# One level of Strassen's algorithm for the two wide products of a SwiGLU block

## The chip, the core and the metric

The kernel runs on one core of a Trainium2 chip. The core has five engines with an instruction stream each: PE (TensorE, matmuls and transposes, results in PSUM), DVE (VectorE), ACT (ScalarE), POOL (GpSimd) and SP (SyncE, which here only issues DMAs). Sixteen DMA engines move data between DRAM and SBUF. The metric is the device time of one execution in microseconds (us), the median over runs. All data are float32.

## What is computed

One decoder block on 512 tokens of 2048 channels. Cut to the parts that matter:

```
h = rmsnorm(x, norm1_g) * (1 + scale1(c)) + shift1(c)
x = x + gate1(c) * (mixer(h) @ w_out)              # mixer begins with h @ w_in
h = rmsnorm(x, norm2_g) * (1 + scale2(c)) + shift2(c)
x = x + gate2(c) * ((silu(h @ w_ff1) * (h @ w_ff3)) @ w_ff2)
out = rmsnorm(x, norm_f_g)
# w_ff1, w_ff3: 2048 x 5632; w_ff2: 5632 x 2048; scale, shift, gate: parts of silu(c) @ w_ada + b_ada
```

The products with w_ff1, w_ff3 and w_ff2 are 70% of the multiplications with large weights.

## The kernel before

A large product is a stream of units (`stream`). A unit is 1 MB of weights, loaded by one DMA on SP's queue into `ws` (2 buffers, pool `wsp`), and 48 matmuls of a 128x128 by a 128x512 tile in 16 steps. Each float32 operand is split in two: a high part that ScalarE casts (L75) and a low part that VectorE subtracts (L76). A product is then three matmuls, high by high, high by low and low by high (`mm3`). While a unit runs, the weights of the next are split, 512 columns after every fourth step, into `wh` and `wl` (5 buffers each); so a load, a cast, a subtraction and the matmuls run beside each other, and the buffers tie them together.

The program has a head (x, the first norm, the first two parts of w_ada, the first columns of w_in), then units for w_in with the mixer in lanes between the steps (`Lane`: small jobs that advance by a step every few steps of the stream), then w_out, then the feed-forward part. `cols_head` loads small rows and transposes them on TensorE (L141) in the head.

The feed-forward part: `open_h2` and `make_h2` transpose x (16 blocks of channels, four transposes each, L1049), scale it by the norm and split it into 16 slots `xh`, `xl`. Four blocks are made before the first product, the other twelve among the first units. `ff_units` then takes 8 (once 4) of the 44 blocks of 128 hidden channels at a time. `block_unit` computes 4 blocks of h @ w_ff1 or h @ w_ff3 with the weights stationary and all 512 tokens moving, 4 units for 512 columns of either weight; the results come out with channels on partitions, go through silu and the product (`d1`, `d3`, L1087) and are split into `hid` (8 buffers in SBUF). Then `row_unit` computes these blocks of hidden @ w_ff2, tokens on partitions, and `add_row` multiplies the sums by the gate and adds them to x (L909, L910) after each group of blocks. In PSUM the eight banks are `row`. The gate's columns, `ada(5, cc)`, run in a lane that begins with the feed-forward part: 16 loads of 256 KB (`wa`) and 16 operations on VectorE for 512 columns. The rstd of the tokens is spread over the partitions by matmuls with a diagonal (`dg`, `rstd_rows`) and applied in `make_h2`.

A scheduler orders each engine's instructions from this program; buffers are tiles of pools, and a tile waits until the last use of the one that had its buffer.

## Time and profile before

| | |
|---|---|
| median of 3 runs | 2545.15 us (2540.65 to 2547.0) |
| span of the profiled execution | 2543.8 us |
| PE busy | 2463.2 us (97%), 14344 matmuls |
| DVE busy | 1441.2 us (57%) |
| ACT busy | 901.1 us (35%) |
| POOL busy | 100.0 us (4%) |
| DMA | 336.32 MB, mean 132 GB/s |

The profiled execution is one of its own, recorded by the hardware profiler; its span runs from its first to its last instruction. Busy times of the engines overlap. Matmuls are pipelined: the busy time of one (0.39 us) is longer than the distance between two, so the price of a matmul is read from a run of many. The stages lie at about 0 to 140 us (head), 140 to 930 us (w_in and the mixer), 930 to 1078 us (the end of the mixer and w_out) and 1086 us to the end (feed-forward).

### The profile page before, as it was taken

To read this page: it belongs to the slowest core of one execution; us is meant where nothing else is said; L and a number is where in the kernel's file an instruction comes from. 1 tells how busy PE (TensorE), PEld (TensorE's weight loads), DVE (VectorE), ACT (ScalarE), POOL (GpSimd) and SP (SyncE) were. 2 spreads that over 40 slices of the span, in tenths; PEclk is the share of its full clock that TensorE was granted. 3 is DMA by queue.
4 is the path that set the end of the run, shared out by engine and by line. 5 is a ranking of instruction groups with operands and counts; after the bars stand their busy time and mean duration, and the time that the engine had idled before them with its cause. 6 is when DMAs were issued, how large, how long until landed. Compare 5 with 4: busy or idle time off the path is not lost.

```text
span 2543.8 us, 35816 instructions
## 1 busy us (share of the span) xinstructions
PE 2463.2 (97%) x14344; PEld 1943.0 (76%) x14344; DVE 1441.2 (57%) x2553; ACT 901.1 (35%) x1461; POOL 100.0 (4%) x157
## 2 busy tenths in 40 slices
PE   6999899999999999999999999999999999999998
PEld 5767666776776767788888888888888888888886
DVE  5765888888988876686343443244324322342345
ACT  4354355356446442342222222222222222222323
POOL 2011110010010000000000000000000000000000
PEclk9999999999999999999999999999999999999999
DMA  9953344344444567556323333322332322233323
GB/s 339 346 164 84 105 117 123 93 125 139 108 107 137 183 207 227 191 190 219 122 91 99 99 100 99 96 88 98 100 99 100 99 90 94 99 100 100 99 98 114
DMA packets 275686, 336.32 MB, mean 132 GB/s; under 512 B 35619, under 2 KB 157713, under 8 KB 274496
## 3 DMA queue, kind: packets, MB, share of 16 engines
...
HBM read 321.41 MB, written 12.58 MB: 131 GB/s over the span
## 4 chain that ended last, share of the span: by engine, by line
PE 85%; DVE 7%; DMA 4%; ACT 2%; issue 1%; POOL 1%; DVEq 0%; ACTq 0%; SPq 0%; POOLq 0%
PE row L67 60%; PE acc L67 14%; PE bk L67 5%; DMA wa<-in_w_ada_dram 3%; PE gg L67 2%; DVE cy L839 1%; DVE wl L76 1%; PE fp L67 1%; PE yy L67 1%; PE first L67 1%; DVE ada L878 1%; DVE tmp L697 0%; ACT L206 0%; DMA dd<-D16d 0%; PE bk L635 0%
## 5 line engine op out<-in xcount | busy, mean ns | idle before, releaser
L76 DVE TENSOR_TENSOR wl<-ws,wh 128x512 fp32r<-128x512 f32 x740 | 519.8, 707 | 847.6 <-ACT wh L75 805.5
L75 ACT CAST wh<-ws 128x512 fp32r<-128x512 f32 x740 | 458.7, 621 | 1288.0 <-PE row L67 1059.7
L67 PE MATMUL row<-xh,wh 128*128 128x512 f32 x1408 | 550.7, 391 | 0.0
L67 PE MATMUL row<-xh,wl 128*128 128x512 f32 x1408 | 548.2, 389 | 0.0
L67 PE MATMUL row<-xl,wh 128*128 128x512 f32 x1408 | 548.1, 389 | 0.0
L67 PE MATMUL row<-wh,hid 128*128 128x512 f32 x1408 | 434.6, 389 | 0.0
L67 PEld LDWEIGHTS row<-xl,wh 128*128 128x128 f32 x1408 | 264.4, 188 | 55.5 <-issue 1.0
L67 PEld LDWEIGHTS row<-xh,wh 128*128 128x128 f32 x1408 | 264.4, 188 | 55.0 <-issue 1.0
L67 PEld LDWEIGHTS row<-xh,wl 128*128 128x128 f32 x1408 | 264.3, 188 | 55.1
L67 PEld LDWEIGHTS row<-wh,hid 128*128 128x128 f32 x1408 | 264.3, 188 | 55.0 <-ACT hid L75 0.2
L67 PE MATMUL row<-wl,hid 128*128 128x512 f32 x704 | 274.0, 389 | 0.0
L67 PE MATMUL acc<-xh,wh 128*128 128x512 f32 x592 | 258.1, 436 | 2.8 <-ACT wh L75 2.8
L67 PE MATMUL acc<-xl,wh 128*128 128x512 f32 x592 | 241.6, 408 | 0.0
L67 PE MATMUL acc<-xh,wl 128*128 128x512 f32 x592 | 239.1, 404 | 0.0
L878 DVE SCALAR_TENSOR_TENSOR ada<-wa,sc,ada 128x512 f32<-128x512 f32 x256 | 191.7, 749 | 52.1 <-DMA wa<-in_w_ada_dram 46.8
L67 PEld LDWEIGHTS row<-wl,hid 128*128 128x128 f32 x704 | 132.2, 188 | 27.4
L67 PEld LDWEIGHTS acc<-xh,wh 128*128 128x128 f32 x592 | 111.9, 189 | 35.1 <-issue 5.1
L67 PEld LDWEIGHTS acc<-xh,wl 128*128 128x128 f32 x592 | 112.4, 190 | 26.5 <-issue 1.9
L67 PEld LDWEIGHTS acc<-xl,wh 128*128 128x128 f32 x592 | 112.5, 190 | 24.7 <-issue 5.7
L206 ACT ACT_TABLE_LOAD x85 | 109.1, 1283 | 2.3 <-PEq L1213 0.8
L839 DVE SCALAR_TENSOR_TENSOR cy<-cu,colC,cy 128x512 f32<-128x512 f32 x120 | 96.6, 805 | 1.7
L839 DVE SCALAR_TENSOR_TENSOR cy<-cu,colD,cy 128x512 f32<-128x512 f32 x120 | 89.2, 744 | 0.6
...
## 6 DMA issues: line engine op xcount, KB each, us to landing
ws<-in_w_ff_dram SPq DMA_DIRECT2D x132, 1024.0 KB, 5.2
wa<-in_w_ada_dram SPq DMA_DIRECT2D x256, 256.0 KB, 3.0
ws<-in_w_in_dram SPq DMA_DIRECT2D x37, 1024.0 KB, 5.9
wa<-in_w_ada_dram SPq DMA_DIRECT2D x32, 1024.0 KB, 11.5
ws<-in_w_out_dram SPq DMA_DIRECT2D x8, 1024.0 KB, 5.1
wa<-in_x_dram SPq DMA_DIRECT2D x4, 1024.0 KB, 6.1
x<-in_x_dram SPq DMA_DIRECT2D x4, 1024.0 KB, 10.7
...
```

The source lines that it names most:

```text
L67: return self.nc.tensor.matmul(out, lhsT=lhsT, rhs=rhs, start=start, stop=stop, skip_group_check=True)
L75: self.nc.scalar.copy(out=hi, in_=x)
L76: self.nc.vector.tensor_tensor(out=lo, in0=x, in1=hi.bitcast(F32), op=ALU.subtract)
L206: self.last_fn = nc.scalar.preload_act_table_set(name).ins
L839: v.scalar_tensor_tensor(out=y, in0=u[:, t:t + T], scalar=self.tap(t, b), in1=y, op0=ALU.mult, op1=ALU.add)
L878: nc.vector.scalar_tensor_tensor(out=acc, in0=was[r], scalar=self.sc[:, r:r + 1], in1=acc, op0=ALU.mult, op1=ALU.add)
```

## The change

The products with w_ff1 and w_ff3 are made by one level of Strassen's algorithm in Winograd's form. The 2 x 2 blocks are: tokens in halves of 256; channels of x in even and odd blocks of 128; columns by weight, 512 of w_ff1 and the same 512 of w_ff3. Seven products of blocks give the four results. In code:

- `make_a`, `make_b` make the sums and differences of x, split (three products' operands in `make_a`, four in `make_b`); x is already scaled by its norm when it is transposed, so the matmuls with the diagonal are gone. Transposes of x stay 64.
- `Fast` is the new unit. It loads 1 MB of w_ff1 (`ws2`, 3 buffers, `WS2`) and 1 MB of w_ff3 (`ws`, 2 buffers) and forms differences of the two on VectorE. Part 0 has 3 products (12 steps, 36 matmuls), part 1 has 4 (16 steps, 48 matmuls); each part has 4 units for 512 columns, and both parts load the same weights. x is now stationary and the weights move. A split is 128x1024 (two blocks of 512) into `pair` (3 buffers of each), started two products ahead.
- `end0`, `end1` combine the products on VectorE and write two of the partial sums back into PSUM, where the products of part 1 add to them. Results have tokens on partitions; `turn` transposes them (16 transposes for 512 columns), splits them and writes both parts to DRAM (`hidd`) through POOL's queue, from the same three buffers `wa` that w_ada uses. The last four blocks stay in SBUF.
- The products with w_ff2 come after all of this, in three passes of 12, 16 and 16 blocks; `back` reads hidden blocks from DRAM through POOL's queue. `add_row` runs after each pass. x goes to DRAM (`x1d`) in the meantime, and `ada(5, cc)` begins with w_ff2.
- The pools of weights lie on the other side of SBUF (`side="right"`).

```diff
+    def bank(self, n):
+        return self.rowp.tile([P, 512], F32, name="b%d" % n, bufs=1)
...
+    def pair(self):
+        return [self.w.tile([P, 2, 512], F32R, name=n, bufs=3) for n in ("wh", "wl")]
...
-        for q in range(4):
-            split(pend[0], q)
+        emit(4)
         while pend:
-            u, _, hi, lo = pend.pop(0)
+            u = pend.pop(0)
             fetch()
...
+            for j in range(u.steps):
+                u.step(j, u.hi, u.lo)
+                emit(u.emit.get(j, 0))
                 yield
...
+        self.x1d = self.dram.tile([T, D], F32, name="x1d")
+        self.hidd = self.dram.tile([NF, 2, P, T], F32, name="hidd")
...
-        self.wsp = self.ctx.enter_context(tc.tile_pool(name="wsp", bufs=1))
+        self.wsp = self.ctx.enter_context(tc.tile_pool(name="wsp", bufs=1, side="right"))
...
+            nc.gpsimd.dma_start(out=self.x1d[t * P:(t + 1) * P, cc * 512:(cc + 1) * 512], in_=x)
...
-                dg = self.ff.tile([P, P], F32, name="dg", bufs=2)
-                self.hold = nc.vector.tensor_scalar(out=dg, in0=self.ident, scalar1=rs, scalar2=None, op0=ALU.mult).ins
-                p = self.row_acc()
-                self.mm(p[:, 0:P], self.ones, dg, True, True)
-                nc.scalar.copy(out=self.RS[:, t * P:(t + 1) * P], in_=p[:, 0:P])
...
+                for c in range(4):
+                    o = self.x1[c][:, t]
+                    if c == 0:
+                        nc.vector.tensor_scalar(out=o, in0=o, scalar1=rs, scalar2=None, op0=ALU.mult)
+                    else:
+                        nc.scalar.activation(out=o, in_=x if c == 3 else o, func=AF.Identity, scale=rs)
...
+        def make_a(kp):
+            raw = f["raw"][kp] = self.xr.tile([P, 4, 256], F32, name="raw", bufs=KB // 2 + 1)
+            for n in range(2):
+                pt = self.bank(6 + n)
+                for t in range(NT):
+                    c0 = (kp % 2) * 256 + n * P
+                    nc.tensor.transpose(out=pt[:, t * P:(t + 1) * P], in_=self.x1[kp // 2][:, t, c0:c0 + P],
+                                        identity=self.ident)
+                k = 2 * kp + n
+                nc.scalar.activation(out=raw[:, n:4:2], in_=pt.rearrange("p (h c) -> p h c", h=2), func=AF.Identity,
+                                     scale=s2[:, k:k + 1], bias=sh2[:, k:k + 1])
+            self.split(*f["x"][kp], raw[:, 0:2].rearrange("p a c -> p (a c)"))
+            d = self.w.tile([P, 512], F32, name="ada")[:, 0:256]
+            nc.vector.tensor_tensor(out=d, in0=raw[:, 0], in1=raw[:, 2], op=ALU.subtract)
+            a = slice((kp % 2) * 256, (kp % 2 + 1) * 256)
+            self.split(*(t[:, a] for t in f["x"][8 + kp // 2]), d)
...
+        def make_b(kp):
+            v = nc.vector
+            raw = f["raw"][kp]
+            if kp % 2 == 0:
+                f["yh"].append(self.xp.tile([P, NT, 512], F32R, name="x1", bufs=4)
+                               .rearrange("p (k a) c -> p k (a c)", k=2))
+            v.tensor_tensor(out=raw[:, 2], in0=raw[:, 2], in1=raw[:, 3], op=ALU.add)
+            v.tensor_tensor(out=raw[:, 0], in0=raw[:, 2], in1=raw[:, 0], op=ALU.subtract)
+            v.tensor_tensor(out=raw[:, 1], in0=raw[:, 1], in1=raw[:, 0], op=ALU.subtract)
+            f["yl"].append(self.xr.tile([P, 4, 256], F32R, name="raw", bufs=KB // 2 + 1)
+                           .rearrange("p a c -> p (a c)"))
+            self.split(f["yh"][kp // 2][:, kp % 2], f["yl"][kp], raw.rearrange("p a c -> p (a c)"))
...
+                def acc(part, q, t, bk=bk):
+                    n = (((0, 4, 2), (4, 0, 2, 6))[part][q]) + t
+                    fresh = part == 0 or q in (0, 3)
+                    if fresh and (part, q, t) not in bk:
+                        bk[part, q, t] = bk[n] = self.bank(n)
+                    return bk[n], fresh
...
+                def end0(j, bk=bk):
+                    sg, us, lo, hi = f["sums"]
+                    q, t = j // 4, j % 2
+                    if j % 4 < 2:
+                        return
+                    if q == 0:
+                        s.copy(out=us[t], in_=bk[t])
+                    elif q == 1:
+                        tt(sg[t], bk[4 + t], us[t], ALU.add)
+                        self.fn(sg[t], sg[t], AF.Silu)
+                    else:
+                        tt(bk[t], us[t], bk[2 + t], ALU.subtract)
+                def end1(j, bk=bk):
+                    sg, us, lo, hi = f["sums"]
+                    q, t = j // 4, j % 2
+                    if j % 4 < 2 or q == 0:
+                        return
+                    if q == 1:
+                        s.copy(out=us[t], in_=bk[t])
+                        tt(hi[t], bk[4 + t], us[t], ALU.add)
+                    elif q == 2:
+                        tt(lo[t], bk[2 + t], hi[t], ALU.add)
+                        tt(lo[t], lo[t], sg[t], ALU.mult)
+                    else:
+                        tt(us[t], bk[6 + t], us[t], ALU.add)
+                        self.fn(us[t], us[t], AF.Silu)
+                        tt(hi[t], hi[t], us[t], ALU.mult)
...
+                def turn(m, dst=None, banks=(6, 7), c=c):
+                    pt = self.bank(banks[m % 2])
+                    for t, x in enumerate(f["sums"][2] + f["sums"][3]):
+                        nc.tensor.transpose(out=pt[:, t * P:(t + 1) * P], in_=x[:, m * P:(m + 1) * P],
+                                            identity=self.ident)
+                    if dst:
+                        self.split(dst[0], dst[1], pt)
+                        return
+                    h, l = (self.w.tile([P, 512], F32, name="wa", bufs=3) for _ in range(2))
+                    self.split(h.bitcast(F32R), l.bitcast(F32R), pt)
+                    for n, x in enumerate((h, l)):
+                        nc.gpsimd.dma_start(out=self.hidd[4 * (c - 1) + m, n], in_=x)
...
+                            if c == 0 and part == 0 and u < 3 and j in (1, 6):
+                                make_a(2 * u + 2 + j // 6)
+                            if c == 0 and part == 0 and u == 3 and j in (7, 9):
+                                make_b(j // 9)
+                            if c == 0 and part == 1 and u < 3 and j in (1, 7):
+                                make_b(2 * u + 2 + j // 7)
+                            if c and part == 0 and u in (1, 2) and j in (1, 6):
+                                turn(2 * (u - 1) + j // 6)
+                            if u == 3:
+                                (end0, end1)[part](j)
+                        x = Fast(self, i["w_ff1"][0], i["w_ff3"][0], part, u, 512 * c, acc, lhs,
+                                 {(0, 0, 0): open_h2, (NF // 4 - 1, 1, 0): open_hid}.get((c, part, u)), stepped)
+                        if (c, part, u) == (NF // 4 - 1, 1, 3):
+                            x.emit = {0: 1, 4: 1, 8: 2, 12: 2}
...
+        KS = [list(range(12)), last4 + list(range(12, 24)), list(range(24, NF - 4))]
+        def back(k):
+            j = f["slot"] = f.get("slot", -1) + 1
+            j %= KB + HB
+            if j < KB:
+                hh[k], hl[k] = self.place(j)
+            else:
+                t = self.ff.tile([P, 2, T], F32R, name="hid", bufs=HB)
+                hh[k], hl[k] = t[:, 0], t[:, 1]
+            if k not in last4:
+                for n, x in enumerate((hh[k], hl[k])):
+                    nc.gpsimd.dma_start(out=x.bitcast(F32), in_=self.hidd[k, n])
+        def open_hid():
+            for k in KS[0]:
+                back(k)
...
+            rest, ks = {}, KS[1][8:] + KS[2]
+            for at, n in (((0, 1, 0), HB), ((0, 3, 4), 4), ((0, 3, 8), 4), ((1, 0, 0), 4), ((1, 3, 8), 4), ((1, 3, 12), 3)):
+                rest[at], ks = ks[:n], ks[n:]
+            assert HB == 5 and not ks
...
+class Fast:
+    def __init__(self, k, w1, w3, part, u, c0, acc, lhs, before=None, stepped=None):
+        self.k, self.part, self.u, self.before = k, part, u, before
+        self.w, self.c0, self.acc, self.lhs, self.stepped = (w1, w3), c0, acc, lhs, stepped
+        n = 4 if part else 3
+        self.steps, self.emit = 4 * n, {4 * j: 1 for j in range(n)}
+        self.hi, self.lo = [], []
+        self.preps = [lambda q=q: self.prep(q) for q in range(n)]
+    def fetch(self):
+        k = self.k
+        self.ws = [k.wsp2.tile([P, D], F32, name="ws2", bufs=WS2), k.wsp.tile([P, D], F32, name="ws", bufs=2)]
+        for t, w in zip(self.ws, self.w):
+            k.load_rows(t, w, range(4 * self.u, 4 * self.u + 4), self.c0)
+    def prep(self, q):
+        k = self.k
+        sub = lambda out, a, b: k.nc.vector.tensor_tensor(out=out, in0=a, in1=b, op=ALU.subtract)
+        (e, o), (E, O) = ([t.rearrange("p (k two c) -> p two k c", two=2, c=512)[:, n] for n in range(2)]
+                          for t in self.ws)
+        if self.part == 0:
+            if q == 2:
+                sub(E, E, O)
+            x = (e, o, E)[q]
+        else:
+            if q == 0:
+                sub(E, E, e)
+                x = E
+            elif q == 1:
+                sub(e, O, E)
+                x = e
+            elif q == 2:
+                x = O
+            else:
+                sub(o, o, e)
+                x = o
+        h, l = k.pair()
+        k.split(h, l, x)
+        self.hi.append(h)
+        self.lo.append(l)
+    def step(self, j, hi, lo):
+        q, kk, t = j // 4, j % 4 // 2, j % 2
+        kp = 2 * self.u + kk
+        h, l = self.lhs(self.part, q, kp)
+        ts = slice(t * P, (t + 1) * P)
+        acc, fresh = self.acc(self.part, q, t)
+        self.k.mm3(acc, h[:, ts], l[:, ts], hi[q][:, kk], lo[q][:, kk], fresh and kp == 0, kp == KB // 2 - 1)
+        if self.stepped:
+            self.stepped(j)
```

SP issues the loads in its own order. In this and the other pieces L is a line of the kernel, out<-in names tiles and inputs, a number behind a name tells tiles of one name apart, and what an instruction waits for is in brackets. The start of SP before:

```order
L368 DMA wa_135<-in_x_dram 128x2048
L135 DMA rows_80<-in_c_dram 16x128 [waits Pool_49]
L135 DMA rows_80<-in_b_ada_dram 96x128
L135 DMA rows_80<-in_norm1_g_dram 16x128
L368 DMA wa_136<-in_x_dram 128x2048
L352 DMA wa_169<-in_w_ada_dram 128x8x256
L352 DMA wa_171<-in_w_ada_dram 128x8x256 [waits DMAHW0_49]
...
L218 DMA ws_1324<-in_w_in_dram 128x16x128 [waits DMAHW7_49]
L218 DMA ws_1326<-in_w_in_dram 128x16x128 [waits DMAHW0_49]
```

and of the changed kernel:

```order
L227 DMA ws_1359<-in_w_in_dram 128x16x128
L142 DMA rows_85<-in_c_dram 16x128 [waits Pool_49]
L142 DMA rows_85<-in_b_ada_dram 96x128
L142 DMA rows_85<-in_norm1_g_dram 16x128
L227 DMA ws_1361<-in_w_in_dram 128x16x128
L360 DMA wa_138<-in_x_dram 128x2048 [waits DMAHW2_49,DMAHW3_49,DMAHW1_49,PE_49]
L360 DMA wa_139<-in_x_dram 128x2048
L344 DMA wa_172<-in_w_ada_dram 128x8x256
```

The first two loads of `ws` (w_in, 1 MB each) have moved from behind the head's loads to its front, and the first load of x now stands behind them and the small rows, and waits for PE.

VectorE while w_ff1 is multiplied, before, where `ws_12329` is one unit's weights and `ws_12399` the next one's:

```order
L76 TENSOR_TENSOR wl_12414<-ws_12329,wh_12413 128x512 [waits DMAHW3_49,PE_49,Activation_49]
L76 TENSOR_TENSOR wl_12430<-ws_12329,wh_12429 128x512 [waits PE_49,Activation_49]
L76 TENSOR_TENSOR wl_12446<-ws_12329,wh_12445 128x512 [waits PE_49,Activation_49]
L76 TENSOR_TENSOR wl_12462<-ws_12329,wh_12461 128x512 [waits PE_49,Activation_49]
L76 TENSOR_TENSOR wl_12480<-ws_12399,wh_12479 128x512 [waits DMAHW4_49,PE_49,Activation_49]
L76 TENSOR_TENSOR wl_12496<-ws_12399,wh_12495 128x512 [waits PE_49,Activation_49]
```

and in the second part of a steady group of the changed kernel, where `ws_13320` with `ws2_13319`, `ws_13395` with `ws2_13394` and `ws_13458` with `ws2_13457` are three units one after the other:

```order
L1389 TENSOR_TENSOR ws_13395<-ws_13395,ws2_13394 128x2x512 [waits DMAHW6_49,DMAHW1_49,DVE_49]
L83 TENSOR_TENSOR wl_13466<-ws_13320,wh_13465 128x1024 [waits Activation_49]
L1389 TENSOR_TENSOR ws2_13394<-ws_13395 128x2x512 [waits DVE_49]
L83 TENSOR_TENSOR wl_13484<-ws2_13319,wh_13483 128x1024 [waits Activation_49]
L1389 TENSOR_TENSOR ws2_13394<-ws2_13394 128x2x512 [waits DVE_49]
L83 TENSOR_TENSOR wl_13501<-ws_13395,wh_13500 128x1024 [waits Activation_49]
L1389 TENSOR_TENSOR ws_13458<-ws_13458,ws2_13457 128x2x512 [waits DMAHW2_49,DMAHW0_49]
L83 TENSOR_TENSOR wl_13519<-ws2_13394,wh_13518 128x1024 [waits Activation_49]
L1389 TENSOR_TENSOR ws2_13457<-ws_13458 128x2x512 [waits DVE_49]
L1389 TENSOR_TENSOR ws2_13457<-ws2_13457 128x2x512 [waits DVE_49]
L83 TENSOR_TENSOR wl_13540<-ws_13395,wh_13539 128x1024 [waits Activation_49]
L83 TENSOR_TENSOR wl_13557<-ws2_13394,wh_13556 128x1024 [waits Activation_49]
```

Splits of one unit after the other became splits of 1024 with the differences of the next units among them; the difference of the third unit stands ahead of splits of the second.

The loads of the same stretch on SP, before, one after the other:

```order
L239 DMA ws_12251<-in_w_ff1_dram 128x4x512 [waits DMAHW0_49,DVE_49]
L239 DMA ws_12329<-in_w_ff1_dram 128x4x512 [waits DMAHW1_49,DVE_49]
L239 DMA ws_12399<-in_w_ff1_dram 128x4x512 [waits DMAHW2_49,DVE_49]
L239 DMA ws_12465<-in_w_ff3_dram 128x4x512 [waits DMAHW3_49,DVE_49]
L239 DMA ws_12531<-in_w_ff3_dram 128x4x512 [waits DMAHW4_49,DVE_49]
```

and in the changed kernel, for the same units (`ws2_13603`, `ws_13604` belong to the next group):

```order
L248 DMA ws2_13394<-in_w_ff1_dram 128x4x512 [waits DMAHW1_49,DVE_49]
L248 DMA ws_13320<-in_w_ff3_dram 128x4x512 [waits DMAHW3_49,DVE_49]
L248 DMA ws2_13457<-in_w_ff1_dram 128x4x512 [waits DMAHW2_49,DVE_49]
L248 DMA ws_13395<-in_w_ff3_dram 128x4x512 [waits DMAHW5_49,DVE_49]
L248 DMA ws_13458<-in_w_ff3_dram 128x4x512 [waits DMAHW7_49,DVE_49]
L248 DMA ws2_13532<-in_w_ff1_dram 128x4x512 [waits DMAHW4_49,DVE_49]
L248 DMA ws_13533<-in_w_ff3_dram 128x4x512 [waits DMAHW1_49,DVE_49]
L248 DMA ws2_13603<-in_w_ff1_dram 128x4x512 [waits DMAHW6_49,DVE_49]
L248 DMA ws_13604<-in_w_ff3_dram 128x4x512 [waits DMAHW2_49,DVE_49]
```

Two loads a unit stand where one stood; the load of w_ff1 of a unit is issued before that of w_ff3 of the unit ahead of it where its buffer comes free earlier.

## Rows read from the trace of the kernel before

**Rows 1.** The page: busy us, share of the span, instructions; granted clock by slice.

```profile
PE 2463.2 (97%) x14344; PEld 1943.0 (76%) x14344; DVE 1441.2 (57%) x2553; ACT 901.1 (35%) x1461; POOL 100.0 (4%) x157
...
PEclk9999999999999999999999999999999999999999
```

**Rows 2.** The chain of waits at its end: start us, us, what.

```profile
1123.24 1401.11 PE row L67 x6173
```

**Rows 3.** The page, costliest groups: count | busy, mean ns | idle.

```profile
L67 PE MATMUL row<-xh,wh 128*128 128x512 f32 x1408 | 550.7, 391 | 0.0
L67 PE MATMUL row<-xh,wl 128*128 128x512 f32 x1408 | 548.2, 389 | 0.0
L67 PE MATMUL row<-xl,wh 128*128 128x512 f32 x1408 | 548.1, 389 | 0.0
```

**Rows 4.** A window: us, busy (count) by engine, clock, DMA share, GB/s.

```profile
1600.00:1800.00 200.00, 200.00 (x884) 165.60 (x884) 74.48 (x114) 51.96 (x85) 0.00 (x0) 1.00 0.29 95
```

**Rows 5.** Waits of the stretch 1108 to 2544: total us, times, longest.

```profile
ACT wh L75 <- PE row L67: 986.0, 489, 2.1
DVE wl L76 <- ACT wh L75: 780.5, 403, 2.9
```

**Rows 6.** Windows of the head and of the stage of w_out.

```profile
60.00:100.00 40.00, 38.26 (x221) 29.29 (x221) 26.81 (x64) 13.45 (x20) 0.00 (x0) 0.96 1.10 347
930.00:970.00 40.00, 38.22 (x157) 29.74 (x157) 22.88 (x34) 12.76 (x24) 0.53 (x1) 0.96 0.73 256
```

**Rows 7.** The head: the chain (two rows), then the timeline of SP and PE.

```profile
0.81 5.40 DMA wa<-in_x_dram
...
118.79 11.75 DMA wa<-in_w_ada_dram
...
2.65 1.39 SPq L368 DMA_DIRECT2D wa<-in_x_dram  x3
...
6.87 0.45 PE L141 MATMUL bk<-ident,rows 128*128 128x128 f32 x1 [6.87 <-POOL rows L131]
...
126.92 5.84 SPq L218 DMA_DIRECT2D ws<-in_w_in_dram  x2
```

**Rows 8.** Timeline of PE, start of the feed-forward part: start us, us.

```profile
1093.85 0.60 PE L1049 MATMUL row<-ident,x 128*128 128x128 f32 x4
...
1097.04 0.60 PE L1049 MATMUL row<-ident,x 128*128 128x128 f32 x4
```

**Rows 9.** Groups of DVE and ACT by shape; last, two subtractions in the timeline.

```profile
L76 DVE TENSOR_TENSOR wl<-ws,wh 128x512 fp32r<-128x512 f32 x518 | 355.9, 692 | 821.2 <-ACT wh L75 780.5 <-PE row L67 40.6
...
L878 DVE SCALAR_TENSOR_TENSOR ada<-wa,sc,ada 128x512 f32<-128x512 f32 x54 | 40.5, 750 | 21.5 <-DMA wa<-in_w_ada_dram 19.5 <-DMA ada<-in_b_ada_dram 1.5
...
L76 DVE TENSOR_TENSOR wil<-wi,wih 128x832 fp32r<-128x832 f32 x16 | 16.3, 1026 | 3.7 <-ACT wih L75 3.3
...
L75 ACT CAST wh<-ws 128x512 fp32r<-128x512 f32 x740 | 458.7, 621 | 1288.0 <-PE row L67 1059.7 <-PE acc L67 192.7 <-PE gg L67 18.3
...
L75 ACT CAST wih<-wi 128x832 fp32r<-128x832 f32 x16 | 14.1, 888 | 4.5 <-PE first L67 4.5
...
136.20 1.29 DVE L76 TENSOR_TENSOR xl<-lo,xh 128x512 fp32r<-128x512 f32 x2 [2.10 <-ACT xh L75]
```

**Rows 10.** DMA issues: queue, count, KB each, median us to landing.

```profile
ws<-in_w_ff_dram SPq DMA_DIRECT2D x132, 1024.0 KB, 5.2
...
x<-in_x_dram SPq DMA_DIRECT2D x4, 1024.0 KB, 10.7
...
mix<-bv SPq DMA_DIRECT2D x7, 256.0 KB, 2.8
...
rows<-in_conv_w_dram POOLq DMA_DIRECT2D x1, 64.0 KB, 5.3
```

**Rows 11.** Timeline of PE from w_out to w_ff1.

```profile
1077.72 0.47 PE L67 MATMUL row<-wh,xl 128*128 128x512 f32 x1
...
1086.54 0.61 PE L67 MATMUL row<-xh,wh 128*128 128x512 f32 x1
```

245 lines of the change are left out of this document (135 added, 110 removed).

## The prediction

> **What bounds the kernel now.** I read the page first: TensorE is busy for 97% of the span, VectorE for 57%, and the granted clock is 0.9 or more of full speed in every slice [rows 1]. The reader should then see in the chain of waits that the last piece is one unbroken run of TensorE, 1401.11 us with 6173 matmuls, from 1123 us to the end [rows 2]. So the stage that the change touches, the products with w_ff1, w_ff3 and w_ff2, is bound by the count of matmuls: 1401.11 / 6173 = 0.227 us each. The page's costliest groups show 1408 matmuls of each of the three forms of ff1 and ff3, 4224 together [rows 3]. In a stretch of 200 us TensorE is busy for all 200, VectorE for 74, and the transfers bring 95 GB/s [rows 4]; ScalarE's casts wait for TensorE (for the buffers of weights) and VectorE's subtractions for ScalarE [rows 5]. Everything but TensorE has room there. It is otherwise in the first 127 us: the sixteen DMA engines are full (a share of 1.10) and bring about 345 GB/s [rows 6], and the chain there is a load of w_ada [rows 7].
>
> **What goes.** Eight products become seven. Per 512 columns of w_ff1 and w_ff3 there were 8 units of 48 matmuls, 384; now four units of 3 x 12 and four of 4 x 12, 336. Over 11 groups that is 528 matmuls fewer, and all lie on the chain: 528 x 0.227 = **-119.9 us**. The matmul keeps its shape (128x128 by 512 columns), so I keep its price.
>
> **Transposes.** The results come out with tokens on partitions, so each group adds 4 x 4 transposes. Before, four transposes stand between every 12 matmuls while the stage starts: from one such row to the next are 1097.04 - 1093.85 = 3.19 us, and 12 x 0.227 = 2.72, so four cost 0.47 us [rows 8]. 44 x 0.47 = **+20.7 us**. They need results that were finished a unit earlier, so I add no wait.
>
> **VectorE in a steady group.** A subtraction of 128x512 lasts 692 ns and two back to back take 1.29 us, a pitch of 0.60; 128x832 lasts 1026 ns [rows 9]. In proportion 128x1024 is an estimate of 1.23 us, at a pitch of 1.13. A group has 28 splits of 1024 and 4 + 12 differences of weights (4 in the first part, 12 in the second), 44 x 1.13 = 49.7, with 14 operations at the ends and 4 splits of turned results, 18 x 0.60 = 10.8: 60 us. TensorE needs 336 x 0.227 + 4 x 0.47 = 78.2 us. VectorE is at 77%; ScalarE's casts (888 ns for 832, so about 1.05 for 1024) come to some 35 us. Neither is the bound by its sum. DMA moves 18.9 MB in these 78.2 us, 242 GB/s, below the 345 that it reached [rows 6].
>
> **The chain through the loads.** The sum hides one loop. In the second part of a group the order on VectorE puts the differences of unit m+2 ahead of splits of unit m+1, and the buffer of w_ff3 that m+2 wants comes free with the third split of unit m. So from one third split to the next there are a load, some 0.3 us of semaphores, and five operations of 1.13: L + 5.95 us, for the 48 x 0.227 = 10.9 us that TensorE works on a unit. A load of 1 MB of these weights lands 5.2 us after its issue [rows 10]; that makes 11.15, 0.28 too many, over three units 0.8 us, which a lead of 1 to 1.7 us (pairs are made two products ahead) may hide. I take 0.7 us for each of nine steady groups, **+6.3**, with 0 to 4 each as bounds: 4 would be a landing of about 6.8, and that of four loads at once is 10.7 [rows 10]. In the first part the loop is L + 2.6 against 8.2 us and holds up to about L = 8 with a lead of 3 us.
>
> **Head.** Two loads of w_in now stand ahead of x on SP, and x's own loads wait for TensorE's first transpose. Before, x went out at 0.81 us, landed 5.40 us later, although three more followed it from 2.65 us on, and that transpose came at 6.87 [rows 7]. While the DMA engines are full, 2 MB put in front cost 2.1 / 0.345 = 6.1 us, and if x only goes out after the transpose, 6 to 8. The two loads used to be issued at 126.92, at the end of this stretch, where products of the head still ran, so nothing is given back. I take **+6.5**, bounds 4 and 9.
>
> **Start of the fast stage.** Between the last product with w_out (1077.72) and the first with w_ff1 (1086.54) lie 8.8 us, most of it the norm of the last tokens and the first transposes [rows 11]. The matmuls with the diagonal go, but scaling of the rows by ScalarE comes before the transposes, three operations of about 0.62 for the last tokens; I take +1.5. In the first group the differences of x come on top: two a unit, each three of 256 and one of 1024, 2.1 us. For three units of the second part VectorE then has 7 x 1.13 + 4.2 = 12.1 us of work for TensorE's 10.9, 3.6 us too many. Together **+5**, bounds 0 and 10.
>
> **Last group and start of ff2.** Into the second part of the last group fall the reading back of 12 blocks (24 loads of 256 KB, 6.3 MB, on POOL's queue), 16 loads for the first gate columns (4.2 MB) and their 16 operations on VectorE, 750 ns each [rows 9]: 28 x 1.13 + 8 x 0.60 + 16 x 0.75 = 48 us for 192 x 0.227 = 43.6 of TensorE, and together with the weights DMA comes near its 345 GB/s. Four or five us of VectorE lie over, and the loads land later. I take **+8**, bounds 0 and 20. What follows, the products with w_ff2, has the same 2112 matmuls; its 28 other blocks read back over 480 us cost nothing while DMA has the room of [rows 4]. The additions into x fall from 96 to 48, beside TensorE, and give nothing.
>
> **Sum.** -119.9 + 20.7 + 6.3 + 6.5 + 5 + 8 = -73.4. The profiled execution has a span of 2543.8 and the median of the runs is 2545.15, 1.35 more. 2543.8 - 73.4 + 1.35 = **2471.8 us**.
>
> **Rivals.**
> A. The writes of hidden blocks hold VectorE. They go through POOL's queue, and the three buffers are shared by four turns, two at a time, 3.9 and 5.2 us apart. A read of 64 KB on that queue landed after 5.3 us [rows 10]; 256 KB is then an estimate of 6 us (SP's writes of that size took 2.8, the lower bound). At 6 us the waits come to some 5 us a group, within the 2 x (9.1 - 5.7) = 6.8 us that VectorE has free in these two units; at 8 us three waits grow by 1.8 and 3.6 us a group are over: 10 x 3.6 = 36, 2508. For: no row shows this queue while VectorE subtracts. Against: DMA engines are not full. The Trainium skill (SBUF — State Buffer, Who interferes with whom) warns that a DMA issued by GpSimd can starve for descriptors while VectorE holds the port that they share, but gives that to VectorE's doubled modes and, with two inputs in SBUF, to GpSimd instructions that read SBUF. By that rule these subtractions do not hold the writes and the sum stays; if the lock did bite, each issue would wait for one operation of 1.13 us and the time would go towards A. No run here shows it.
> B. Weight loads land after 7 us because other transfers share the engines. The loop is then 12.95 us, 3 x 2.07 less the lead of 1.6 is 4.6 a group, 11 x 4.6 = 51 in place of 6.3: 2516. For: DMA's rate rises from 95 to 242 GB/s. Against: in a stretch of the stage of w_out DMA moves 256 GB/s and TensorE is busy for 38.22 of 40 us [rows 6], and x's first load was not held up by those behind it.
> C. Slower than before: these loads land as the four of x did, 10.7 us. The loop is 16.65 us, 3 x 5.8 - 1.6 = 15.7 a group, 172 in all: 2638. It decides from where a group loses (73.4 + 6.3) / 11 = 7.25 us, which is L = 7.9. Against: those four were issued together, and here one or two are under way.
> D. Nothing stalls and the head costs its lower bound: -119.9 + 20.7 + 4 = -95, 2450.
> E. The change does not do what it says, in that splits do not run ahead: a difference, a cast and a split in a row are 1.13 + 1.05 + 1.23 = 3.4 us for a product of 2.72, 0.7 x 77 = 53, 2520. The order shows differences ahead of the splits, which speaks against it.
>
> **Chances.** Forecast 0.61 (its own range 2455 to 2495), A 0.10, B 0.11, C 0.08, D 0.06, E 0.04. The range from 2448 to 2520 takes in all but C and half of the edges. A measurement of this kernel can tell about 0.3% from no change; within that are 2537 to 2553, between B and C. Faster by more 0.88, within 0.03, slower 0.09.
>
> **What would show it.** The chain after should again be one run of TensorE from the first group on, with a pitch of 0.227. A steady group should last about 79 us. If differences of 128x2x512 wait for DMA on w_ff for more than some us a group, it is B or C; if splits of `wa` wait for DMA on `hidd`, A. Landings of w_ff near 5.2 make the forecast right, above 7 wrong. The first product with w_in should come 4 to 9 us later. A granted clock below 0.9 in the stage would overturn the price of every matmul.

## The result, and the profile after

| | before | after |
|---|---|---|
| median | 2546.07 us (4 runs, 2540.65 to 2548.13) | 2563.07 us (4 runs, 2559.0 to 2566.28) |
| ratio | | 1.0067, interval 1.0051 to 1.0083 |
| span of the profiled execution | 2543.8 | 2559.1 |

The change makes the kernel slower by 0.7%. The forecast was 2472 with a range of 2448 to 2520, so the time lies outside the range and has the other sign. The sum in the prediction gives a span of 2470.4; 88.7 us are to be found.

The page of the kernel after, its busy times and the granted clock in 40 slices, which answer to [rows 1]:

```profile
PE 2433.8 (95%) x13984; PEld 1874.1 (73%) x13984; DVE 1782.8 (70%) x2723; ACT 1038.6 (41%) x1493; POOL 196.4 (8%) x333
...
PEclk9999999999999999999999999999999999999999
```

The count of matmuls fell as it should (13984 for 14344, transposes included), the granted clock is 0.9 or more in every slice, as before (its mean over the span is 0.981, for 0.989), and TensorE is busy for 95%. Yet the time that the stage takes hardly fell: from the first product with w_ff1 to the last with w_ff2 it was 1086.54 to 2532.1 before, 1445.6 us; it is 1113.6 to 2547.2 now, 1433.6. That is 12 us less, where -119.9 and the terms that the prediction set against it inside the stage (+20.7, +6.3, +3.6, +8) gave -81.3.

**The matmul itself became dearer.** A stretch of the products with w_ff2, in which nothing was changed but where the operands lie; first before, then after (columns as in [rows 4]: stretch, its length, busy time and count of each engine, granted clock, DMA share, GB/s):

```profile
2200.00:2500.00 300.00, 300.00 (x1325) 248.44 (x1325) 118.01 (x182) 83.67 (x144) 0.00 (x0) 1.00 0.30 97
```

```profile
2200.00:2500.00 300.00, 300.00 (x1284) 241.23 (x1284) 104.05 (x164) 66.41 (x124) 7.47 (x14) 1.00 0.31 106
```

TensorE is busy for all 300 us in both, the granted clock is 1.00 in both, and DMA is idle for two thirds. But 1284 matmuls fit in where 1325 did: 0.2336 us each for 0.2264. In runs of 48 matmuls without a gap the mean distance is 0.234 us in this stage and 0.2343 in the products with w_ff1 and w_ff3, for 0.2267 before (the sum took 0.227 from [rows 2]). So the cost is 3696 x 0.0076 = 28.1 us in ff1 and ff3 and 2112 x 0.0073 = 15.4 in ff2: **43.5 of the 88.7 us**. The products with w_out have it too (48 in 11.25 us), but there no time hangs on it: in e5 and e7 below, where the distance is 0.227 again, the last product with w_out starts at 1102.26 and 1102.09, for 1100.41 here.

**Waits from the first product with w_ff1 on.** Eight steady groups, by the same view, which answer to [rows 4]:

```profile
1210.00:1850.00 640.00, 628.15 (x2724) 502.59 (x2723) 482.16 (x476) 280.70 (x308) 34.68 (x64) 0.99 0.68 229
```

The waits from 1090 to 2080 us, about the whole part with w_ff1 and w_ff3 (columns: engine, what waited, for whom; us in total, times, the longest):

```profile
ACT wh L82 <- PE b L71: 368.6, 234, 5.4
DVE ws L1389 <- DMA ws<-in_w_ff_dram: 102.0, 54, 4.7
...
DVE wa L83 <- DMA hidd<-wa: 39.2, 15, 3.9
...
PE b L71 <- DVE wl L83: 19.3, 8, 7.5
```

Before, no wait of this part reached TensorE: ScalarE waited for TensorE, VectorE for ScalarE [rows 5]. Now VectorE waits 102 us for weights (54 times) and 39 us for buffers `wa` whose writes to `hidd` have not landed (15 times). Most of it is covered; 19.3 us come through to TensorE by way of the split weights `wl`. One group, VectorE and then TensorE (start, duration, what it is, idle time before it and who ended it):

```profile
1381.66 1.23 DVE L1389 TENSOR_TENSOR ws<-ws 128x1024 f32<-128x1024 f32 x1 [3.30 <-DMA ws<-in_w_ff_dram]
...
1387.24 0.69 DVE L83 TENSOR_TENSOR wa<-b,wa 128x512 fp32r<-128x512 f32 x1 [1.49 <-DMA hidd<-wa]
...
1393.73 1.22 DVE L1389 TENSOR_TENSOR ws<-ws,ws 128x1024 f32<-128x1024 f32 x1 [4.67 <-DMA ws<-in_w_ff_dram]
```

```profile
1397.41 0.50 PE L71 MATMUL b<-wl,xh 128*128 128x512 f32 x1 [3.43 <-DVE wl L83]
```

All three waits lie in the *first* part of the group (1375 to about 1400), in which the sixteen DMA engines are nearly full, unlike in its second part:

```profile
1375.00:1380.00 5.00, 5.00 (x24) 4.07 (x23) 2.08 (x3) 2.69 (x3) 1.08 (x2) 1.00 0.95 315
1385.00:1390.00 5.00, 5.00 (x23) 4.04 (x22) 2.58 (x3) 2.35 (x3) 1.54 (x3) 1.00 0.94 280
1400.00:1440.00 40.00, 39.87 (x171) 31.94 (x170) 31.21 (x30) 16.45 (x18) 0.00 (x0) 1.00 0.55 189
```

The four `turn`s of the group before stand in two of the four units there, so 2 MB of writes fall on top of the loads. The writes issued from 1380 to 1386 landed after 8.5 us (median of three; 5.8 over the whole run), the three buffers `wa` came free late, the splits of the turned results waited, and behind them on VectorE the differences and splits of weights. The nine steady groups lose 17.1 us (periods 80.5 to 84.5 us, where 336 x 0.2343 + 4 x 0.47 = 80.6 is without waits), the first group some 0.8. The last group loses 10.3 us and the start of ff2 some 18, the longest of it in these two rows of TensorE, a wait for split weights and one for the gate's columns:

```profile
1982.47 0.79 PE L71 MATMUL b<-wl,xh 128*128 128x512 f32 x1 [7.45 <-DVE wl L83]
```

```profile
2181.59 1.22 PE L71 MATMUL b<-ada,ones 128*128 128x512 f32 x1 [8.97 <-DVE ada L870]
```

Such a wait costs more than its length. For 4 us after the first of these two, and for about 6 after the second, the granted clock is 0.50 (the level of 1.2 GHz) and the matmuls are 0.427 us apart:

```profile
1983.00:1984.00 1.00, 1.00 (x4) 0.74 (x3) 0.96 (x2) 0.28 (x1) 0.00 (x0) 0.50 0.99 367
```

Together 46 us for a forecast of 18: **28 us**.

**Before the first product with w_ff1.** It starts at 1113.58 for 1086.54 [rows 11], 27 us later where 8 were forecast, so **19 us** more. The starts of products in the two traces tell where: 5.9 us at the first product of the units with w_in (157.80 for 151.92), 10.8 more by the first with w_out (883.45 for 866.80), 6.0 more by the last with w_out (1100.41 for 1077.72), and 4.4 more in the step from there to w_ff1 (13.2 us for 8.8, where 1.5 more was forecast). At the start of w_out TensorE was busy for 38.22 of 40 us [rows 6], and is now for 29.51:

```profile
930.00:970.00 40.00, 29.51 (x103) 21.43 (x101) 24.72 (x39) 15.33 (x26) 2.73 (x5) 0.87 0.80 279
```

Its two waits there:

```profile
948.37 0.61 PE L71 MATMUL acc<-wh,xh 128*128 128x512 f32 x1 [3.11 <-ACT xh L82]
...
957.41 0.80 PE L71 MATMUL b<-wh,xh 128*128 128x512 f32 x1 [4.44 <-DVE tm L901]
```

Not all of this is lost, since before TensorE waited at other places of this stage: its waits from 860 to 1080 add up to 11.0 us, those from 880 to 1101 now to 12.4. e10 and e11 below ask what slows w_in and w_out. In the step to w_ff1 the longest wait of TensorE is that of the transposes of x:

```profile
1111.62 1.97 PE L1079 MATMUL b<-ident,x 128*128 128x128 f32 x8 [3.51 <-ACT raw L1082]
```

### The profile page after: what moved, and what is told of

It reads as the page before. It is cut to its first block, busy times and chain, and to the rows that moved or that the text cites. A ratio compares the mean times of both kernels' runs of the same rounds, so it can differ in the third digit from the quotient of the medians.

```text
span 2559.1 us, 35669 instructions
## 1 busy us (share of the span) xinstructions
PE 2433.8 (95%) x13984; PEld 1874.1 (73%) x13984; DVE 1782.8 (70%) x2723; ACT 1038.6 (41%) x1493; POOL 196.4 (8%) x333
## 4 chain that ended last, share of the span: by engine, by line
PE 48%; issue 32%; DVE 10%; DMA 5%; POOL 3%; ACT 2%; POOLq 0%; SPq 0%; DVEq 0%; ACTq 0%
PE b L71 24%; PE acc L71 14%; PE bk L71 5%; DMA wa<-in_w_ada_dram 3%; DVE cy L831 2%; DVE wl L83 2%; PE gg L71 2%; POOL hidd L1168 2%; PE first L71 1%; PE fp L71 1%; DVE ada L870 1%; DVE tmp L689 1%; PE yy L71 1%; DVE xl L692 1%; DMA ws<-in_w_ff_dram 0%
## 5 line engine op out<-in xcount | busy, mean ns | idle before, releaser
L82 ACT CAST wh<-ws 128x512 fp32r<-128x512 f32 (+1 forms) x696 | 548.9, 810 | 1018.4 <-PE b L71 780.8
L83 DVE TENSOR_TENSOR wl<-ws,wh 128x512 fp32r<-128x512 f32 (+1 forms) x696 | 644.1, 941 | 299.0 <-ACT wh L82 297.9
L71 PE MATMUL b<-wl,xh 128*128 128x512 f32 x1232 | 493.8, 401 | 19.3 <-DVE wl L83 19.3
L71 PE MATMUL b<-wh,xh 128*128 128x512 f32 x1232 | 500.3, 406 | 4.4 <-DVE tm L901 4.4
L71 PE MATMUL b<-wh,xl 128*128 128x512 f32 x1232 | 492.1, 399 | 0.0
L71 PEld LDWEIGHTS b<-wl,xh 128*128 128x128 f32 x1232 | 235.1, 191 | 79.5 <-DVE wl L83 23.4
L71 PE MATMUL b<-wh,x 128*128 128x512 f32 x704 | 279.8, 397 | 0.7
L71 PE MATMUL b<-wl,x 128*128 128x512 f32 x704 | 279.2, 397 | 0.0
L71 PE MATMUL b<-wh,raw 128*128 128x512 f32 x704 | 279.1, 396 | 0.0
L71 PEld LDWEIGHTS b<-wh,xl 128*128 128x128 f32 x1232 | 234.8, 191 | 57.4 <-issue 0.2
```

The lines of the kernel that those rows point to most:

```text
L71: return self.nc.tensor.matmul(out, lhsT=lhsT, rhs=rhs, start=start, stop=stop, skip_group_check=True)
L82: self.nc.scalar.copy(out=hi, in_=x)
L83: self.nc.vector.tensor_tensor(out=lo, in0=x, in1=hi.bitcast(F32), op=ALU.subtract)
```

## Experiments

Two questions stood after the traces: what makes one and the same matmul cost 0.234 us in place of 0.2267, and which of several changes causes the waits. For the first, what differs is where the operands lie in SBUF; the change moves the pools of weights to the other side, and the addresses of the built kernels show that `wh` and `wl` are then no more at the same place within 256 bytes as x is.

**e1_pad32.** The kernel after, with 32 bytes in front of the weights' pools.

```diff
+        pad = self.ctx.enter_context(tc.tile_pool(name="pad", bufs=1, side="right"))
+        nc.gpsimd.memset(pad.tile([P, 8], F32, name="pad"), 0.0)
```

> The changed kernel with one unused tile of 32 bytes a partition put first on the right side of SBUF: wh, wl, ws, ws2 and wa move from addresses that are 32 above a multiple of 64 to multiples of 64, as wh and wl were in the kernel before. Nothing else changes. Theory P (place): a matmul costs 0.234 us instead of 0.227 wherever wh or wl lies 32 off, so here the pitch is 0.227 again in every stage: 3696 x 0.0076 + 2112 x 0.007 + 768 x 0.007 + about 10 us in the stage of w_in = 58 us less than the change, some 2505 us, unless waits grow where TensorE becomes faster (then 2505 to 2520). Rival T (traffic): the pitch is longer because VectorE, ScalarE and DMA read and write more beside TensorE; then it stays 0.234 and the time stays at 2563. Rival S (shape): it is due to the pair tiles of 128x2x512 or to x being stationary; also 0.234 and 2563.

Measured: 2552.86 us, ratio 1.0024 (1.0010 to 1.0038), 10 us faster than the kernel after. The distance fell, but only to 0.2325 us in ff1 and ff3 and, in the mean, 0.2315 in ff2. So the place matters, but a place that is a multiple of 64 bytes is not what counts.

**e2_before_shift.** The kernel before, with 32 bytes in front of the pool `w` (and 32 behind it, so that what follows moves by 64).

```diff
+        pad = self.ctx.enter_context(tc.tile_pool(name="pad", bufs=1))
+        nc.gpsimd.memset(pad.tile([P, 8], F32, name="pad"), 0.0)
         self.w = self.ctx.enter_context(tc.tile_pool(name="w", bufs=1))
+        pad = self.ctx.enter_context(tc.tile_pool(name="pad2", bufs=1))
+        nc.gpsimd.memset(pad.tile([P, 8], F32, name="pad2"), 0.0)
```

> The kernel before with 32 unused bytes ahead of the pool of wh and wl and 32 behind it, so that these alone lie 32 above a multiple of 64; order, shapes and traffic stay. Theory P: the pitch goes from 0.227 to about 0.234 where wh and wl are stationary (w_in, w_ff1, w_ff3) and where they move (w_out, w_ff2); 6336 x 0.007 + 768 x 0.007 + about 10 = 60 us more than before, some 2605 us. If only one of the roles counts, the pitch changes in its stages alone: moving, 2112 + 768 matmuls, 20 us more; stationary, 4224 and w_in, 40 us more. Rivals T and S: no change, 2546 us.

Measured: 2588.46 us, 1.0165 (1.0149 to 1.0180). The same stretch of 300 us:

```profile
2200.00:2500.00 300.00, 300.00 (x1287) 241.67 (x1287) 106.76 (x163) 78.55 (x128) 0.00 (x0) 1.00 0.29 95
```

1287 matmuls for 1325: 32 bytes that hold nothing make the large products of the kernel *before* nearly as dear as after, with the weights stationary (ff1, ff3: 0.2333) and with the weights moving (w_out and ff2: 0.2333). So the price rises without stationary x, the new block shapes and the new traffic; that these add nothing of their own is shown by e5. The built kernel shows that the hidden blocks moved along, from 64 to 128 above a multiple of 256, so in ff2 both operands moved; in the other stages the weights alone did. The first product with w_ff1 comes at 1085.50, for 1086.54 before: up to there the dearer matmul costs nothing.

**e3_spread.** e1 with the four turns spread, one in each unit of the first part.

```diff
-                            if c and part == 0 and u in (1, 2) and j in (1, 6):
-                                turn(2 * (u - 1) + j // 6)
+                            if c and part == 0 and j == 6:
+                                turn(u)
```

> As e1_pad32, with the four turns of a group one in each unit of the first part, at its seventh step, instead of two in the second and two in the third unit. It tells what the waits of TensorE at the last unit of the first part come from (0 to 3.6 us a group, 13 us over groups 1 to 9). Theory W: writes of hidden blocks (2.1 MB within 17 us) and the loads of weights fill the DMA engines together, loads land after 9 to 10 us, and VectorE waits for them in its order; spread over 34 us the waits go, 10 to 15 us less than e1_pad32. Rival O: the waits come from the order of differences and splits alone; no more than 3 us change.

Measured: 2535.29 us, 0.9953 (0.9935 to 0.9971), 17.6 us less than e1. The eight steady groups:

```profile
1210.00:1850.00 640.00, 640.00 (x2823) 519.84 (x2822) 507.57 (x498) 290.38 (x321) 34.55 (x64) 1.00 0.69 237
```

TensorE is busy for all 640 us, a group lasts 79.8, and the writes to `hidd` land after 2.6 us in place of 5.4 in e1. The whole wait of the steady groups was turns that crowd into two units.

**e4_wa4.** e1 with a fourth buffer for the turned results.

```diff
-                    h, l = (self.w.tile([P, 512], F32, name="wa", bufs=3) for _ in range(2))
+                    h = self.w.tile([P, 512], F32, name="wa", bufs=3)
+                    l = self.w.tile([P, 512], F32, name="ada") if m % 2 else self.w.tile([P, 512], F32, name="wa", bufs=3)
```

> As e1_pad32, with a fourth buffer for turned results (the tile of the gate sums, unused there), so that a turn never waits for the write of the turn just before it; the amount and the time of the writes stay. Rival A of the prediction (VectorE and ScalarE wait for writes through the three shared buffers): 8 to 13 us less than e1_pad32. Theory W (DMA is full, the loads are late): no more than 4 us less.

Measured: 2547.17 us, 0.9996 (0.9980 to 1.0011), 5.7 less than e1; groups of 80.1 to 81.3 us for e1's 80.1 to 82.3. The lack of a buffer alone is the smaller part; the crowd of transfers and of work on VectorE in these units is the rest.

**e5_place.** e1 with 160 bytes for the 32, and 192 in front of the hidden blocks of ff2, so that weights, x and hidden blocks all lie at 64 within 256 bytes.

```diff
-        nc.gpsimd.memset(pad.tile([P, 8], F32, name="pad"), 0.0)
+        nc.gpsimd.memset(pad.tile([P, 40], F32, name="pad"), 0.0)
...
+            nc.gpsimd.memset(self.ff.tile([P, 48], F32, name="pad2", bufs=1), 0.0)
```

> As e1_pad32, but 160 unused bytes in place of 32, and 192 ahead of the hidden blocks of the last stage. In the kernel before, the weights wh, wl and what they are multiplied with (slots of x, hidden blocks) all lie 64 above a multiple of 256 bytes; in the change wh and wl lie 224 above one, in e1_pad32 192, the slots 64, hidden blocks of the last stage 128. Here all lie 64 above again. e1_pad32 left a pitch of 0.229 to 0.232 us between 0.227 and 0.234. Theory R (relative place): the rest of the loss comes from the two operands not lying alike within 256 bytes; then the pitch is 0.227 in w_out, w_ff1, w_ff3 and w_ff2, and 3696 x 0.005 + 2112 x 0.004 + 768 x 0.004 + some 5 us of w_in = 35 us less than e1_pad32, 2518 us. Theory T (the rest is traffic or shape): no change, 2553.

Measured: 2531.6 us, 0.9940 (0.9917 to 0.9963). The distance is 0.2267 us in ff2 and 0.227 in w_out, ff1 and ff3:

```profile
2200.00:2500.00 300.00, 300.00 (x1325) 248.47 (x1324) 112.64 (x178) 70.53 (x134) 7.44 (x14) 1.00 0.32 109
```

But it is 21 us less than e1 and not the 35 expected, since a faster TensorE meets the crowded turns sooner: the nine steady groups lose 24 us, in e1 10. Eight of them, by the same view:

```profile
1210.00:1850.00 640.00, 629.98 (x2794) 515.76 (x2793) 496.90 (x494) 288.85 (x318) 34.54 (x64) 0.99 0.69 235
```

**e6_before128 and e12_before256.** The kernel before, shifted as in e2 by 128 and by 256 bytes (the tiles `[P, 8]` are `[P, 32]` and `[P, 64]`).

> The kernel before with 128 unused bytes ahead of the pool of wh and wl and 128 behind it: they lie on multiples of 64 still, but 192 above a multiple of 256, as in e1_pad32, while slots of x and hidden blocks stay 64 above one. Theory R: pitch about 0.230 to 0.232, some 6336 x 0.004 + 5 = 25 to 35 us slower than before, 2571 to 2581. Theory T, or that multiples of 64 are all that counts: 0.227 and 2546.

> The kernel before with 256 unused bytes ahead of the pool of wh and wl and 256 behind it: weights, slots and hidden blocks all lie 64 above a multiple of 256 again, at another place. Theory R (only the relative place within 256 bytes counts): pitch 0.227 everywhere, the time of before within 0.3%. Rival M (any move of these buffers costs, for instance by the place against other tiles or by a longer stretch than 256): pitch 0.230 to 0.234 and 2575 to 2590 us, as with 32 and 128 bytes.

Measured: 2586.81 us, 1.0163 (1.0148 to 1.0178), for 128 bytes; 2546.66 us, 1.0002 (0.9992 to 1.0011), for 256. The 300 us of each:

```profile
2200.00:2500.00 300.00, 300.00 (x1288) 241.36 (x1287) 106.74 (x163) 78.66 (x129) 0.00 (x0) 1.00 0.28 95
```

```profile
2200.00:2500.00 300.00, 300.00 (x1326) 248.39 (x1325) 117.94 (x183) 84.35 (x144) 0.00 (x0) 1.00 0.30 97
```

A shift by 256 bytes costs nothing, so it is neither the shift as such nor the padding. The built kernels and their distances (address of a tile within a partition, modulo 256; mean us from matmul to matmul). In e1 and in the kernel after, 32 of the 44 hidden blocks lie in the slots of x, at 64, and 12 in other tiles, at 128; ff2 then has a distance for either:

| kernel | `wh`, `wl` | x | hidden | ff1, ff3 | ff2 |
|---|---|---|---|---|---|
| before; e12 | 64 | 64 | 64 | 0.2267 | 0.2267 |
| e5, e7, e9 | 64 | 64 | 64 | 0.227 | 0.2267 |
| e1 | 192 | 64 | 64; 128 | 0.2325 | 0.2326; 0.2293 |
| e6 | 192 | 64 | 64 | 0.233 | 0.233 |
| e2 | 96 | 64 | 128 | 0.2333 | 0.2333 |
| after | 224 | 64 | 64; 128 | 0.2343 | 0.2343; 0.2334 |

Where both operands of the products lie at the same place modulo 256, the matmul costs 0.2267 us; elsewhere 0.229 to 0.2343. In e1 the same weights at 192 cost 0.2326 us with hidden blocks at 64 and 0.2293 with those at 128, so it is not the place of the weights alone. That only the difference counts, and not the place 64 itself, was not tried, and what in the memory makes it is open.

**e7_place_spread.** e5 and e3 together.

> e5_place and the spread turns of e3_spread together. By theory R and the 17.6 us that e3_spread took off e1_pad32: about 2518 - 17 = 2500 us, a steady group of 336 x 0.227 + 4 x 0.47 = 78.2 us; if a faster TensorE brings back waits for the loads, up to 10 us more. By theory T: 2535, as e3_spread.

Measured: 2507.09 us, 0.9851 (0.9831 to 0.9871). The steady groups hold 2887 matmuls and transposes in the 640 us in which the kernel after had 2724:

```profile
1210.00:1850.00 640.00, 639.83 (x2887) 529.30 (x2886) 512.43 (x505) 297.67 (x328) 36.16 (x67) 1.00 0.70 244
```

The two causes together are 56 us of the 88.7.

**e8_hold.** e7, with the loads of the gate's columns held back until the last group is done.

```diff
+            with self.tc.issue_after(self.hold) if self.hold and r < 2 else nullcontext():
                 nc.sync.dma_start(out=wa, in_=self.i["w_ada"][0, r * P:(r + 1) * P, c0:c0 + 512])
...
-                        tt(hi[t], hi[t], us[t], ALU.mult)
+                        self.hold = tt(hi[t], hi[t], us[t], ALU.mult).ins
```

> As e7_place_spread, with the gate's first operation on VectorE held behind the last operation of the last group. In e3_spread TensorE waits 7.0 us in the last group, 4.7 us before the last blocks are transposed, and 10.8 us for the gate at the end of the first columns of w_ff2. Theory G (the gate's loads and sums, moved ahead by the scheduler, hold buffers, VectorE and SP's queue in the last group): the 7 and the 4.7 go, and the wait for the gate becomes at most 7 longer: 5 to 11 us less than e7_place_spread. Rival: the 7 us come from hidden blocks being read back at that time; then nothing goes there and the gate comes later, 0 to 10 us slower.

Measured: 2514.44 us, 0.9879 (0.9863 to 0.9896), 7 us *more* than e7. A wait of 5.1 us stays in the last group (e7: 6.0), and those for the gate in ff2 grow from 6.7 to 18.7 us. The gate's loads are not what holds the last group. In e7 VectorE waits there for the weights themselves, while POOL issues the reading back of twelve blocks:

```profile
1932.28 1.22 DVE L1392 TENSOR_TENSOR ws<-ws 128x1024 f32<-128x1024 f32 x1 [10.08 <-DMA ws<-in_w_ff_dram]
```

**e9_ends.** e7 with the ends mended: the head's order and place as before, the twelve blocks read back four at a time behind differences of weights in the last group, and the gate's steps closer together.

```diff
-        rows = tmp.enter_context(self.tc.tile_pool(name="rows", bufs=1))
+        rows = tmp.enter_context(self.tc.tile_pool(name="rows", bufs=1, side="right"))
...
-        self.load(self.ws)
+        with self.k.tc.issue_after(self.k.behind.pop()) if self.k.behind else nullcontext():
+            self.load(self.ws)
...
+            m = nc.gpsimd.tensor_copy(out=self.mark[:, 8 * u:8 * u + 8], in_=e[:, 0, 0:8]).ins
+            with tc.issue_after(m):
+                for k in KS[0][4 * u - 4:4 * u]:
+                    back(k)
...
+ADA5 = (2, 1) + (2,) * 20
```

> e7_place_spread with three edits in places apart from each other. Head: the small rows lie on the right side, so that the first load of x does not wait for their transpose, and the two loads of w_in go out behind the head's; if that order is what the head lost, the first product with w_in comes 6 us earlier, at about 152 us as before. Last group: the first 12 hidden blocks are read back four at a time in the last three units of its second part, where before the scheduler let them go while the first part still ran; in e7_place_spread VectorE waits 10.1 us there for a load of w_ff3 and TensorE 6.1. Theory W (transfers on POOL's queue make the loads of weights late): the 6.1 us go, and no more than 2 of them come back in the second part. Gate: its lane takes 43 steps for 512 columns in place of 50, where the first pass of w_ff2 has 48; the wait of 8.6 us at the end of that pass (6.9 + 0.8 + 1.0) goes. Together 20 us less than e7_place_spread, some 2487 us; if the last group only changes the place of its waits, 2493.

Measured: 2497.07 us, 0.9797 (0.9774 to 0.9819), the fastest of all here, but 10 us less than e7 and not the 20 expected. The first product of the units with w_in comes at 151.39 us (before 151.92, e7 158.34); of these 7 us, 3.7 are left at the first with w_ff1 (1113.20, e7 1116.86). The first rows of SP after, and of e9:

```profile
0.81 0.44 SPq L227 DMA_DIRECT2D ws<-in_w_in_dram  x1
...
8.01 1.94 SPq L360 DMA_DIRECT2D wa<-in_x_dram  x4
```

```profile
0.81 0.39 SPq L361 DMA_DIRECT2D wa<-in_x_dram  x1
```

In the kernel after, x waits until 8.01 because its tile lies on the memory of the small `rows`, which are transposed first; with `rows` elsewhere x goes out at once. The order of the loads of w_in was put back in the same run, so how much each of the two gives is not separated. The wait of the last group only moved: 5.0 and 2.0 us in its last units, and 2.5 before the last blocks are transposed.

**e10_before_pairs.** The kernel before with its splits in pairs, as `pair` has them: 3 buffers of two halves for 5 of one (and `tm` with 2 buffers for 4, to make room).

```diff
-            h = self.w.tile([P, 512], F32R, name="wh", bufs=5)
-            l = self.w.tile([P, 512], F32R, name="wl", bufs=5)
+            if q % 2 == 0:
+                self.pair = [self.w.tile([P, 2, 512], F32R, name=n, bufs=3) for n in ("wh", "wl")]
+            h, l = (t[:, q % 2] for t in self.pair)
```

> The kernel before with the changed kernel's buffers of weights: wh and wl as three pairs of 512 columns, taken and given back two at a time, in place of five single ones (and two in place of four buffers tm in the last stages, for room). The changed kernel takes some 10 us more between its first product with w_in and the last, with the pitch as before in e7_place_spread too. Theory Q (pairs): a pair comes free only when both halves are used up, so that splits run less far ahead: 8 to 12 us more in that stage here (915.0 us before, at the 1920th of the products with w_in by the trace). Rival H: the 10 us come from the later start of the head, which moves the mixer's loads and lanes against the stream; here less than 3 us.

Measured: one run, 2558.55 us, for 2547.24 of the kernel before beside it. The start of w_out, and the first product with w_ff1:

```profile
930.00:970.00 40.00, 28.66 (x94) 20.39 (x93) 22.96 (x35) 14.41 (x24) 0.53 (x1) 0.79 0.72 262
```

```profile
951.62 0.80 PE L67 MATMUL row<-wh,xh 128*128 128x512 f32 x1 [6.24 <-DVE tm L910]
```

```profile
1099.67 0.50 PE L67 MATMUL row<-xh,wh 128*128 128x512 f32 x1
```

TensorE is busy for 28.66 of the 40 us, as in the kernel after (29.51), and the first product with w_ff1 comes 13.1 us later than before, without any Strassen. The kernel is 9.0 us behind at the first product with w_out already (875.84 for 866.80), where nothing has used `tm` yet. A pair comes free only when both its halves are used, so the splits run less far ahead. The wait in w_out shown here is one for `tm`, of which this kernel has 2 and the kernel after 3, so what the pairs cost in the last 4 us is not separated.

**e11_singles.** e9, with each of the six buffers taken alone in the old units, the high and the low part of one split in one buffer.

```diff
-        if q % 2 == 0:
-            self.pair = self.k.pair()
-        h, l = (t[:, q % 2] for t in self.pair)
+        t = self.k.w.tile([P, 2, 512], F32R, name=("wh", "wl")[q % 2], bufs=3)
+        h, l = t[:, 0], t[:, 1]
```

> e9_ends with the buffers of weights used one by one in the units of w_in, w_out and w_ff2: the same six tiles of 128x2x512, each now for the high and the low part of one split of 512 columns, in place of two splits in two tiles; the units of w_ff1 and w_ff3 keep theirs. e10_before_pairs lost 9 us between the first and the 1920th product with w_in and as many at the start of w_out, of which 13 remain before w_ff1. Theory Q (pairs come free too late): the same goes here, the last product with w_out comes 12 to 18 us earlier, 2497 - 14 = some 2483 us. Rival: the changed kernel's loss there has other causes (x1 loaded by columns, the pools' places); less than 4 us change, 2494 to 2500.

Measured: 2498.78 us, 0.9817 (0.9800 to 0.9833), no different from e9. The first products with w_ff1, of e9 and of e11:

```profile
1113.20 0.79 PE L71 MATMUL b<-wh,xh 128*128 128x512 f32 x1
```

```profile
1103.09 0.80 PE L71 MATMUL b<-wh,xh 128*128 128x512 f32 x1
```

The 10 us are won where they were lost, and half of them is given back: in the profiled executions the last product with w_ff2 comes 5.4 us earlier than in e9 (2481.06 for 2486.47), the steady groups take 2.9 us more, ff2 3.5 more and the last group 2.3 less. By the medians nothing is left of them; why stays open. Nor are the pairs all of the late start: e11 reaches w_ff1 16.5 us later than the kernel before, and TensorE is still busy for only 31.25 of the 40 us from 930 on. The step from w_out to w_ff1 has 6.3 of these (15.1 us for 8.8); for the other 10 no run shows a cause.

## Why the prediction was wrong, by its own steps

- **What goes, -119.9: the step that failed.** The count was right (528 fewer), the price not: "The matmul keeps its shape (128x128 by 512 columns), so I keep its price." The price hung on where the operands lie, 0.2343 and 0.234 us for 0.2267; 43.5 us lost. Stationary x was not the cause (e2: the same with either role), nor the clock (1.00 in both stretches), which I had named as the one thing that could overturn the price. The diff showed `side="right"`, and I gave it no term. e2, e5, e6 and e12 show this cause, and e5 gives it back.
- **Transposes, +20.7:** no row contradicts it; a steady group of e3 and e7 has no time left over. **VectorE in a steady group:** the estimate of 1.23 us for 128x1024 was right (1.22).
- **The chain through the loads, +6.3:** 17.1. I looked for the loop in the second part, and it held there; it was in the first part that loads and turns met. There I took L + 2.6 us against 8.2 with nothing else on DMA or on VectorE. The term was mis-sized and in the wrong place; e3 shows that spreading the turns removes all of it.
- **Rival A** saw the right place, the three buffers, and a landing of 6 us (5.8 measured), but let VectorE's free time cover it. It was a small share (e4: 5.7 us). The Trainium skill (SBUF — State Buffer, Who interferes with whom) limits the starving of GpSimd's DMAs to VectorE's doubled modes and, with two inputs in SBUF, the lock to GpSimd's own reads of SBUF; the trace agrees: with VectorE busy for 482.16 of 640 us the writes landed after 5.8 us, and in e3 with VectorE busier (507.57) after 2.6. **B and C:** the loads' median stayed at 5.2 us, as forecast; neither came about. My two signs disagreed here: VectorE waited 102 us in eleven groups for the weights, which I had called the sign of B or C, yet most of that was covered. **E** was priced too low, 77 products where eleven groups have 308 (seven products in each of four units); nothing of its kind came about, since a steady group of e7 takes the 78.1 us of its matmuls and transposes.
- **Head, +6.5:** 5.9. Size right, and that x waits for the first transpose; the reason is the shared memory of `rows` (e9).
- **Start of the fast stage, +5:** 5.2, but by luck: the step from w_out to w_ff1 lost 4.4 us for 1.5, the first group 0.8 for 3.6. And the 16.8 us lost in w_in and w_out were no term at all: I read "3 buffers of each" as more room (six halves for five) and not that a pair comes free as a whole. That is worth 9 to 13 us in e10 and 10 in e11; the rest is open. The rows at the start of w_out that I used against rival B [rows 6] are a place where TensorE stood still afterwards.
- **Last group and start of ff2, +8:** 28. The bound of 20 was too low, and the half clock after a long wait had no term. e8 shows that the gate's loads do not cause the wait in the last group; e9 and e11 moved it about without removing it.

By size: 43.5 price, 28 waits in the stage, 19 before it; that is 1.8 more than the 88.7, since the sum took 0.227 where 0.2267 was measured (5808 x 0.0003 = 1.7). With the first put right and nothing else, e5 took 2531.6 us: faster than before, as forecast, but still above the range, and the third stands in e7 and e9 too.
